# Hymba encoder block: attention and output projection given out in larger groups

## The chip, the cores and the metric

The kernel runs on one core of one Trainium2 chip. The metric is the device time of one execution in microseconds, lower is better; the time before is the median of three runs. The engines are PE (TensorE: matrix products and transposes; its weight loads are shown as PEld), DVE (VectorE), ACT (ScalarE), POOL (GpSimd) and SP (SyncE, which issues most of the DMAs).

## The reference

The reference is one encoder layer over 16 meta tokens and 1024 real tokens of width 1024. Cut to what matters here:

```
u    = rms_norm(h);  proj = u @ w_in            # q, k, v, z of both groups
o_dn = gated delta rule, forward and backward, 4 heads of 128, 16 chunks of 64 and their reversed copy
o_at = softmax(q k^T) v with rope, 8 query heads, 2 key/value heads, head size 64
h    = h + rms_norm(concat(o_dn, o_at) @ w_out) # the output projection
h    = h + rms_norm(square(relu(rms_norm(h) @ w_up)) @ w_down)
```

The output is h without the meta tokens, in float32.

## The kernel before

All values are kept at about float32 accuracy by writing an operand as a high and a low part: a product is then three matmuls (high by high, high by low, low by high). The program is written out in one long order, and each engine runs its own instructions strictly in that order, so the order in which Python emits the work is the schedule.

The order of everything up to the feed-forward part is made by a small planner, `progress` (L1538). Each piece of work is a generator; a `yield` is a place where the planner may go over to another one. The planner keeps a clock `T.t` that counts only matmuls and transposes (the class `Clock`: columns / 2400 us, four times that for float32). After a yield a generator is due again at `T.t` plus the number that it yielded, or plus its entry in `LAT` (L79: chain 2.2, wout 2.4, qk 0.2, pv 0.2, u2 0.22, proj 0.18 us). Of those that are due the first in the list `URGENCY` (L74) is taken: chain0, chain1, wout, wload, then the spawned `post` pieces, then qt, qk, pv, u2, proj, wup. If none is due, the clock jumps to the first that will be.

The generators around the change:

- `chain` (L1065, twice, for the two directions): the recurrence of the delta rule, 8 steps each. A step has five groups of four float32 products of 128x128, each of which waits for what DVE or ACT made of the one before.
- `qk_head` (L1243), driven by `qk_stream` (L1193): the scores of one head of one 128-row tile, S = 128x1024, as two halves of 512 columns, each a product with KH and one with KL. S has `SB` = 2 buffers in PSUM. Then DVE takes the minimum of S (L1254), and the spawned `softmax` (L1259) lets ACT make the exponential (L1262) and the high part in float16 (L1268), POOL and DVE the low part (L1270, L1271), and SP transposes both by DMA into pT (L1274, `PTB` = 3 buffers). No more than `INF` = 6 heads are under way, and a head's scores come at least `TS_` = 2.55 planner us behind the second last one's.
- `pv_head` (L1284), driven by `pv_stream` (L1204) at least `TP_` = 13.8 planner us behind the scores: for each of 8 key tiles three float16 matmuls of 64 or 65 columns into the PSUM tile o, so 24 for a head, with yields behind the third and the sixth key tile (9, 9 and 6 matmuls). Behind every fourth head 12 more for the meta tokens, then DVE divides (L1309, L1310). There are 64 heads in all (8 tiles of 8).
- `proj_stream` (L1387): for each of 8 tiles of 128 rows, `mix` (L1364) transposes the attention's rows (AQ) and the delta rule's (on) on PE, one tile ahead; then two halves of 512 columns with 24 matmuls each by `mm3` (L250), which yields behind every second of its eight triples (6 matmuls). ACT squares the sums (L1406), DVE scales them (L1414), adds x (L1415), and `norm_rows` makes the next layer's rows u. `mix` of a tile waits for the tile's eight attention heads.
- `u2_stream` (L1477) starts when the last attention tile is done. It has 23 pieces of four transposes each (`u_part`, L1430), which turn the rows u and their sums and differences into the operands of the feed-forward products; five of them for each pair of tiles wait for the later tile's projection. Their row loads (L1444) stand in SP's queue.
- `wout_stream` (L1334) loads and splits w_out's first half behind the end of both chains; the projection starts behind it.

Behind the planner comes the feed-forward part, written as a fixed loop, in which PE has matmuls of 512 columns without a break.

Of the kernel before, what the change touches and what calls it, by code (L numbers as in the profile page):

```python
# [81 lines left out]
def body(tc, I, out, dbg=None):  # L82
# [29 lines left out]
    def tmp(dt=F32):  # L112
        return tp.tile([P, LT + 4], dt, name="t4", tag="t4")

    def psr():
        return psa.tile([P, 512], F32, name="a", tag="a")
# [4 lines left out]
    def small(n, name, bufs=4):  # L121
        return sp.tile([P, n], F32, name=name, tag=name, bufs=bufs)

    def junk():
        return sp.tile([P, D], BF16, name="junk", tag="junk", bufs=1)

    def bc(ap, m):
        return ap.unsqueeze(2).broadcast_to([ap.shape[0], ap.shape[1], m])
# [28 lines left out]
    def rsqrt(dst, src, mult, add, n):  # L157
        r = dst.shape[0]
        ms = sp.tile([P, 16], F32, name="ms", tag="ms", bufs=4)
        V.tensor_scalar(ms[:r, :n], src, float(mult), float(add), ALU.mult, ALU.add)  # L160
        G.tensor_tensor(dst, ms[:r, :n], mhalf[:r, :n], ALU.pow)  # L161
# [14 lines left out]
    def mark(name, after=0.0):  # L176

        done[name] = T.t + after
# [71 lines left out]
    def mm3(ps, pairs, every=100):  # L250

        n = len(pairs)
        for i, (ah, al, bh, bl) in enumerate(pairs):
            T.matmul(ps, lhsT=ah, rhs=bh, start=i == 0, stop=False)
            T.matmul(ps, lhsT=ah, rhs=bl, start=False, stop=False)
            T.matmul(ps, lhsT=al, rhs=bh, start=False, stop=i == n - 1)
            if (i + 1) % every == 0 and i + 1 < n:
                yield
# [5 lines left out]
    def norm_rows(dst, X, r, nrow):  # L264
        ss = small(1, "ss")
        A.activation(junk()[:r], X, AF.Square, accum_out=ss[:r])
        rs = small(1, "rs")
        rsqrt(rs[:r], ss[:r], 1.0 / D, EPS, 1)
        V.scalar_tensor_tensor(dst, X, rs[:r, 0:1], nrow[:r], ALU.mult, ALU.mult)  # L269
# [14 lines left out]
    def spawn(name, g):  # L284

        def w():
            yield from g
            live.remove(name)
        live.append(name)
        at = next((i for i, s in enumerate(st) if s[0] in ("gemm", "qt", "qk")), len(st))  # L290
        st.insert(at, [name, w(), LAT[name], 0.0, 0])
# [584 lines left out]
    def need(*names):  # L876
        while not all(n_ in done for n_ in names):
            yield True
        t = max(done[n_] for n_ in names)
        if t > T.t:  # L880
            yield t - T.t
# [322 lines left out]
    def pv_stream():  # L1204
        for n, (t, h) in enumerate(HEADS):
            while len(tq) <= n:
                yield True
            yield until(tq[n] + TP_)
            while h not in boxes[t]:
                yield True  # L1210
            yield from pv_head(h, boxes[t])
            tp_.append(T.t)
# [30 lines left out]
    def qk_head(t, h, qs, sm, mm, box):  # L1243
        kv = h // 4
        ap_, KH, KL = R["at"], R["KH"], R["KL"]
        s = R["ps"].tile([P, L], F32, name="S", tag="S", bufs=SB)
        for half in range(2):
            sl = slice(half * 512, (half + 1) * 512)
            for i, K_ in enumerate((KH, KL)):
                T.matmul(s[:, sl], lhsT=qs[:, h], rhs=K_[:, kv, sl], start=i == 0, stop=i == 1)  # L1250
            if half == 0:
                yield
        mx, nb = small(1, "mx"), small(1, "nb")
        V.tensor_reduce(mx, s, AX.X, ALU.min)  # L1254
        V.tensor_scalar(nb, mx, mm[:, h:h + 1], UP15, ALU.min, ALU.add)  # L1255
        spawn("post", softmax(t, h, s, sm, nb, box))
        yield

    def softmax(t, h, s, sm, nb, box):  # L1259
        yield SM[0]  # L1260
        p32 = tmp()
        A.activation(p32[:, :L], s, AF.Exp, bias=nb, scale=-1.0)  # L1262
        g, j = divmod(h, 4)
        pm = R["PM"][(2 * t + g) % 3]
        A.activation(pm[:, j * NM:(j + 1) * NM], sm[:, h * NM:(h + 1) * NM], AF.Exp, bias=nb, scale=-1.0)
        yield SM[1]
        p16 = R["P16"][(t * NQ + h) % P16N]
        A.copy(p16[:, 0], p32[:, :L])  # L1268
        yield SM[2]
        G.tensor_tensor(p16[:, 1, :LH], p32[:, :LH], p16[:, 0, :LH], ALU.subtract)  # L1270
        V.tensor_tensor(p16[:, 1, LH:], p32[:, LH:L], p16[:, 0, LH:], ALU.subtract)  # L1271
        yield SM[3]
        pT = R["at"].tile([P, 16, P], F16, name="pT", bufs=PTB)
        S.dma_start_transpose(pT, p16.rearrange("p a b -> p (a b)"))  # L1274
        box[h] = pT
        if j == 3:
            ps = psr()[:, :P]
            T.transpose(ps, pm, idf)
            mh, ml = (R["at"].tile([P, P], F16, name=n, bufs=2) for n in ("pmh", "pml"))
            A.copy(mh, ps)  # L1280
            V.tensor_tensor(ml, ps, mh, ALU.subtract)
            box["m", g] = mh, ml

    def pv_head(h, box):  # L1284
        VP, VM = R["VP"], R["VM"]
        t, pT, osb = box["t"], box.pop(h), box["osb"]
        kv, j = divmod(h, 4)
        W = 1 + HD
        if j == 0:
            box["o"] = R["ps"].tile([P, 512], F32, name="o", tag="o", bufs=1)  # L1290
        ob = box["o"][:, :4 * W]

        def term(o, ph, pl, v, first, last):
            T.matmul(o, lhsT=ph, rhs=v[:, :W], start=first, stop=False, skip_group_check=True)
            T.matmul(o[:, 1:], lhsT=ph, rhs=v[:, W:], start=False, stop=False, skip_group_check=True)
            T.matmul(o, lhsT=pl, rhs=v[:, :W], start=False, stop=last, skip_group_check=True)

        for k in range(NT):
            term(ob[:, j * W:(j + 1) * W], pT[:, k], pT[:, 8 + k], VP[:, k, kv], j == 0 and k == 0, False)
            if k in (2, 5):  # L1300
                yield
        if j == 3:
            while ("m", kv) not in box:
                yield True
            mh, ml = box.pop(("m", kv))
            for i in range(4):
                term(ob[:, i * W:(i + 1) * W], mh, ml, VM[:, kv, i], False, i == 3)
            ov, den = ob.rearrange("p (h c) -> p h c", h=4), box["den"][:, h - 3:h + 1]
            V.reciprocal(den, ov[:, :, 0])  # L1309
            V.tensor_tensor(osb[:, h - 3:h + 1], ov[:, :, 1:], bc(den, HD), ALU.mult)  # L1310
        if h == NQ - 1:
            mark(f"att{t}", 2.5)
        yield
# [48 lines left out]
    WORD = (4, 5, 6, 7, 0, 1, 2, 3)  # L1362
# [24 lines left out]
    def proj_stream():  # L1387
        mixes = {}
        yield from need("wout", "att0")
        mixes[0] = mix(0)  # L1390
        yield
        wout, npost = R["wout"], R["npost"]
        for c in range(NT):
            if c + 1 < NT:
                yield from need(f"att{c + 1}")
                mixes[c + 1] = mix(c + 1)
                yield
            mh, ml = mixes.pop(c)
            xr = tmp()
            S.dma_start(xr[:, :D], x[c * P:(c + 1) * P])  # L1400
            s2, pso = small(2, "s1", 2), []
            for n in range(2):
                sl = slice(n * 512, (n + 1) * 512)
                pso.append(psr())
                yield from mm3(pso[n], [(mh[:, k], ml[:, k], wout[k][0][:, sl], wout[k][1][:, sl]) for k in WORD], 2)
                A.activation(junk()[:, sl], pso[n], AF.Square, accum_out=s2[:, n:n + 1])  # L1406
                yield
            rs = small(1, "rs")
            V.tensor_tensor(rs, s2[:, 0:1], s2[:, 1:2], ALU.add)
            rsqrt(rs, rs, 1.0 / D, EPS, 1)  # L1410
            hx = tmp()
            for n in range(2):
                sl = slice(n * 512, (n + 1) * 512)
                V.scalar_tensor_tensor(hx[:, sl], pso[n], rs[:, 0:1], npost[:, sl], ALU.mult, ALU.mult)  # L1414
            V.tensor_tensor(hx[:, :D], hx[:, :D], xr[:, :D], ALU.add)  # L1415
            A.dma_start(hscr[c * P:(c + 1) * P], hx[:, :D])
            if c == 0:
                yield from need("gain")
            norm_rows(xr[:, :D], hx[:, :D], P, R["npre"])
            if c < 6:  # L1420
                A.dma_start(uscr[c * P:(c + 1) * P], xr[:, :D])
            else:
                held[c] = xr
            mark(f"u{c}", 4.0)
            yield
# [406 lines left out]
    for i in range(7):  # L1832
# [17 lines left out]
        for p in range(together):  # L1850
            n = i * NP_ + p
# [39 lines left out]
```

## Time and profile before

| what | value |
|---|---|
| median of 3 runs | 1415.5 us (1413.3 to 1420.03) |
| the profiled execution | 1416.07 us, its span 1414.2 us |
| granted TensorE clock, mean of the span | 0.979 |
| PE busy | 1342.7 us (95%) |
| DVE, ACT, POOL busy | 1029.3 us (73%), 835.5 us (59%), 295.4 us (21%) |

The span is 1.9 us shorter than the execution, which has a start and an end around it. The stages can be told by what PE works on: input projections, convolutions and the inverses of the delta rule up to about 430 us, the chain together with attention up to about 586 us, attention alone while w_out is loaded up to about 616 us, the output projection together with the rest of attention up to about 748 us, the last of the projection to 774 us, a passage to the feed-forward part up to about 806 us, and that part to the end. A matmul's length in the timeline is its time through the array; matmuls overlap, so the time that one costs PE is read from its start to the start of the next.

### The profile page before, as it was taken

The numbers are of one execution on the slowest core, as the hardware profiler recorded it, in microseconds if no ns is written. First come the engines' busy times: TensorE is split into PE (matmuls) and PEld (weight loads), VectorE is DVE, ScalarE is ACT, GpSimd is POOL, SyncE is SP. The second block draws the span as 40 slices with busy tenths as digits, with TensorE's granted clock in tenths as the row PEclk, the third lists the DMA queues.
The fourth block names the chain that finished last, engine by engine and source line by source line (L and its number), as shares of the span: only waits on it lengthen the run. The fifth ranks groups of instructions, "written<-read, shape, count | busy, mean of one in ns | idle before, by whom it ended". The sixth has DMA issues, their size and how long they took to land. (4 is left out here: it accounts for less than half of the span.)

```text
span 1414.2 us, 26476 instructions
## 1 busy us (share of the span) xinstructions
PE 1342.7 (95%) x9627; PEld 1027.1 (73%) x9627; DVE 1029.3 (73%) x1962; ACT 835.5 (59%) x1747; POOL 295.4 (21%) x386
## 2 busy tenths in 40 slices
PE   6999999999998998899998799999999999999996
PEld 6999888777998877677777444444444888888875
DVE  5636779788768979877765987777775588675675
ACT  6556565756546777866644676666665455445552
POOL 1210234343534456533321200000000000000000
PEclk9999999999998999889999799999999999999998
DMA  6312234344379999997994354444443984466341
GB/s 209 87 57 62 83 98 158 112 149 153 121 253 282 245 264 239 221 242 186 224 225 135 102 175 158 153 155 150 158 155 114 331 271 127 142 193 194 98 150 66
DMA packets 273355, 236.86 MB, mean 167 GB/s; under 512 B 147484, under 2 KB 201656, under 8 KB 273224
## 3 DMA queue, kind: packets, MB, share of 16 engines
q1 hardware_dynamic: 270056, 225.73, 55.3%
q10 hardware_dynamic: 3168, 9.44, 1.8%
q8 instruction: 76, 1.25, 0.4%
q14 instruction: 55, 0.45, 0.1%
HBM read 132.27 MB, written 69.28 MB: 143 GB/s over the span
## 5 line engine op out<-in xcount | busy, mean ns | idle before, releaser
L95 PEld LDWEIGHTS <-wh 128*128 128x128 f16 x896 | 88.1, 99 | 102.7 <-issue 1.9
L95 PE MATMUL a<-woah 128*128 128x512 f32 x672 | 158.6, 390 | 1.3 <-DVE woah L1734 1.2
L95 PE MATMUL a<-woal 128*128 128x512 f32 x672 | 157.4, 389 | 0.0
L95 PEld LDWEIGHTS a<-woah 128*128 128x128 f32 x672 | 125.9, 188 | 29.0 <-DVE woah L1734 2.0
L95 PEld LDWEIGHTS a<-woal 128*128 128x128 f32 x672 | 126.1, 188 | 26.2
L95 PE MATMUL a<-uh,wh 128*128 128x344 f32 (+2 forms) x340 | 122.3, 360 | 0.7 <-ACT cw L665 0.5
L1270 POOL TENSOR_TENSOR P<-t,P 128x640 f16<-128x640 f32 x64 | 99.4, 1555 | 106.8 <-ACT P L1268 85.0
L95 PE MATMUL a<-ul,wh 128*128 128x344 f32 (+2 forms) x340 | 118.7, 349 | 0.5 <-DVE ul L262 0.5
L95 PE MATMUL a<-uh,wl 128*128 128x344 f32 (+2 forms) x340 | 118.3, 348 | 0.0
L161 POOL TENSOR_TENSOR rs<-ms,mhalf 128x1 f32<-128x1 f32 (+1 forms) x33 | 19.1, 578 | 424.0 <-DVE rs L1797 304.6
L1254 DVE TENSOR_REDUCE mx<-S 128x1 f32<-128x1024 f32 x64 | 77.9, 1219 | 24.3 <-PE S L95 24.1
L1262 ACT ACTIVATE t<-S,nb 128x1024 f32<-128x1024 f32 x64 | 71.5, 1117 | 40.8 <-DVE nb L1255 29.2
L95 PEld LDWEIGHTS <-pT 128*128 128x128 f16 x1536 | 59.5, 100 | 42.0 <-issue 26.6
L95 PE MATMUL o<-VP,pT 128*128 128x65 f16 (+1 forms) x1536 | 73.6, 198 | 11.3 <-DMA pT<-P 9.8
L95 PEld LDWEIGHTS <-wl 128*128 128x128 f16 x448 | 43.9, 98 | 54.1 <-issue 1.7
L1731 ACT ACTIVATE woah<-fr,isf 128x512 fp32r<-128x512 f32 x54 | 39.2, 725 | 70.3 <-PE a L95 61.0
L1731 ACT ACTIVATE woal<-fr,isf 128x512 fp32r<-128x512 f32 x54 | 39.2, 726 | 68.4 <-PE a L95 66.2
L1268 ACT CAST P<-t 128x1024 f16<-128x1024 f32 x64 | 66.8, 1043 | 4.7 <-DVE t L269 1.8
L1733 DVE SCALAR_TENSOR_TENSOR woah<-fr,isf,woah 128x512 fp32r<-128x512 f32 x54 | 40.5, 751 | 37.2 <-ACT woah L1731 37.1
L95 PE MATMUL S<-KH,qs 128*128 128x512 f32 x128 | 61.0, 476 | 6.5 <-ACT t L1262 6.5
L95 PEld LDWEIGHTS a<-uh,wh 128*128 128x128 f32 x340 | 65.0, 191 | 2.5 <-ACT cw L665 0.7
L95 PEld LDWEIGHTS a<-ul,wh 128*128 128x128 f32 x340 | 65.1, 192 | 2.1 <-DVE ul L262 1.0
(508 smaller groups left out, 3776.8 us busy)
## 6 DMA issues: line engine op xcount, KB each, us to landing
fr<-fscr SPq DMA_DIRECT2D x108, 256.0 KB
fscr<-os SPq DMA_DIRECT2D x64, 256.0 KB
rb<-in_w_down SPq DMA_DIRECT2D x64, 256.0 KB
fscr<-of SPq DMA_DIRECT2D x48, 256.0 KB
wr<-in_w_in SPq DMA_DIRECT2D x44, 256.0 KB
AQ<-in_w_up SPq DMA_DIRECT2D x22, 512.0 KB
raw<-in_w_up SPq DMA_DIRECT2D x10, 512.0 KB
X<-in_x SPq DMA_DIRECT2D x8, 512.0 KB
```

The lines of the kernel that those rows point to most:

```text
L95: nc.tensor.matmul(out, lhsT=lhsT, rhs=rhs, **kw)
L161: G.tensor_tensor(dst, ms[:r, :n], mhalf[:r, :n], ALU.pow)
L1254: V.tensor_reduce(mx, s, AX.X, ALU.min)
L1262: A.activation(p32[:, :L], s, AF.Exp, bias=nb, scale=-1.0)
L1268: A.copy(p16[:, 0], p32[:, :L])
L1270: G.tensor_tensor(p16[:, 1, :LH], p32[:, :LH], p16[:, 0, :LH], ALU.subtract)
L1731: A.activation(ah, fr, AF.Copy, scale=isf[:, p:p + 1])
L1733: V.scalar_tensor_tensor(al, fr, isf[:, p:p + 1], ah.bitcast(F32), ALU.mult, ALU.subtract)
```

## The change

Three lines go or change, all of them places where the planner may go over to other work. The scores of a head lose the yield between their halves, so that their four matmuls of 512 columns come in one go. The values of a head lose the yields behind the third and the sixth key tile, so that their 24 matmuls come in one go. The projection yields behind every fourth triple instead of every second one, so that its matmuls come in twelves. No instruction is added, removed or altered; their order changes, also on the other engines and in the DMA queues, since the planner decides anew at every yield.

```diff
@@ qk_head
             for i, K_ in enumerate((KH, KL)):
                 T.matmul(s[:, sl], lhsT=qs[:, h], rhs=K_[:, kv, sl], start=i == 0, stop=i == 1)
-            if half == 0:
-                yield
         mx, nb = small(1, "mx"), small(1, "nb")
@@ pv_head
         for k in range(NT):
             term(ob[:, j * W:(j + 1) * W], pT[:, k], pT[:, 8 + k], VP[:, k, kv], j == 0 and k == 0, False)
-            if k in (2, 5):
-                yield
         if j == 3:
@@ proj_stream
-                yield from mm3(pso[n], [(mh[:, k], ml[:, k], wout[k][0][:, sl], wout[k][1][:, sl]) for k in WORD], 2)
+                yield from mm3(pso[n], [(mh[:, k], ml[:, k], wout[k][0][:, sl], wout[k][1][:, sl]) for k in WORD], 4)
```

## Rows read from the trace of the kernel before

**Rows 1.** Busy time of each engine by stage; columns as the header says

```profile
core 0: us, PE busy (x) PEld busy (x) DVE busy (x) ACT busy (x) POOL busy (x), PEclk, DMA share, GB/s
436.00:586.00 150.00, 137.85 (x1570) 120.10 (x1569) 131.51 (x287) 111.49 (x239) 82.56 (x61) 0.97 1.08 242
586.00:616.00 30.00, 23.53 (x242) 18.57 (x239) 24.22 (x38) 23.78 (x36) 13.84 (x11) 0.72 1.08 261
616.00:748.00 132.00, 124.20 (x1159) 94.94 (x1155) 88.70 (x163) 75.10 (x130) 42.16 (x34) 1.00 0.90 214
774.00:806.00 32.00, 19.17 (x94) 13.47 (x93) 29.29 (x48) 20.88 (x40) 10.26 (x9) 0.73 0.24 82
```

**Rows 2.** PE's timeline in the projection: start us, us, instruction, count [idle before <-releaser]

```profile
701.99 0.45 PE L95 MATMUL o<-VP,pT 128*128 128x65 f16 x9
702.27 0.48 PE L95 MATMUL a<-woah,mh 128*128 128x512 f32 x1
702.59 0.40 PE L95 MATMUL a<-woal,mh 128*128 128x512 f32 x1
...
703.75 0.36 PE L95 MATMUL o<-VP,pT 128*128 128x65 f16 x6
...
706.17 0.48 PE L95 MATMUL S<-KH,qs 128*128 128x512 f32 x1
706.49 0.40 PE L95 MATMUL S<-KL,qs 128*128 128x512 f32 x1
706.73 0.45 PE L95 MATMUL o<-VP,pT 128*128 128x65 f16 x9
```

**Rows 3.** PE's timeline: first and last of the runs of values' matmuls

```profile
455.52 1.50 PE L95 MATMUL o<-VP,pT 128*128 128x65 f16 x24
...
744.46 0.90 PE L95 MATMUL o<-VP,pT 128*128 128x65 f16 x24
```

**Rows 4.** ACT's group of exponentials, 586 to 616 us: count | busy us, mean ns | idle before

```profile
L1262 ACT ACTIVATE t<-S,nb 128x1024 f32<-128x1024 f32 x8 | 8.9, 1110 | 2.3 <-DVE nb L1255 1.8 <-POOL P L1270 0.5
```

**Rows 5.** ACT's groups of a head, 616 to 748 us

```profile
L1262 ACT ACTIVATE t<-S,nb 128x1024 f32<-128x1024 f32 x22 | 24.6, 1116 | 20.0 <-DVE nb L1255 12.3 <-issue 2.1 <-DVE ml L1378 1.8
L1268 ACT CAST P<-t 128x1024 f16<-128x1024 f32 x23 | 24.0, 1042 | 3.4 <-DVE t L269 1.8 <-DVE ml L1378 1.6
L1265 ACT ACTIVATE PM<-sm__9520,nb 128x16 f32<-128x16 f32 x8 | 2.4, 302 | 0.2 <-DVE nb L1255 0.2
```

**Rows 6.** Waits, 424 to 780 us: total us, times, longest

```profile
PE o L95 <- DMA pT<-P: 9.8, 8, 2.4
...
PE a L99 <- DVE t L1414: 5.1, 5, 1.5
```

**Rows 7.** PE's timeline at two tile boundaries and the projection's end

```profile
731.39 0.66 PE L99 MATMUL a<-c_id,on 128*128 128x128 f32 x4 [0.85 <-DVE t L1414]
...
747.31 0.66 PE L99 MATMUL a<-c_id,on 128*128 128x128 f32 x4 [1.33 <-DVE t L1414]
...
752.54 0.60 PE L99 MATMUL a<-c_id,urow 128*128 128x128 f32 x4
...
773.65 0.40 PE L95 MATMUL a<-wobh,ml 128*128 128x512 f32 x1
773.89 1.47 PE L99 MATMUL a<-c_id,urow 128*128 128x128 f32 x12
781.04 3.65 PE L99 MATMUL a<-c_id,urow 128*128 128x128 f32 x16 [5.68 <-DVE urow L1455]
```

**Rows 8.** DVE's and SP's timelines behind the projection's end

```profile
777.15 1.41 DVE L1414 SCALAR_TENSOR_TENSOR t<-a,rs,npost 128x512 f32<-128x512 f32 x2 [0.18 <-POOL rs L161]
785.09 0.68 DVE L1438 TENSOR_TENSOR t2l<-a,t2h 128x512 f16<-128x512 f32 x1
785.69 0.68 DVE L1438 TENSOR_TENSOR t1l<-a,t1h 128x512 f16<-128x512 f32 x1
763.14 21.89 SPq L1444 DMA_DIRECT2D urow<-uscr  x8
```

## The prediction

> **What bounds the kernel now.** I read the windows by stage first, then PE's timeline, then the waits. The change acts where attention runs, so the reader looks at the stages and not at the shares of the whole span. In [rows 1] the third column is the stretch's length and the next is PE's busy time. With the chain beside attention (436 to 586 us) PE is busy 137.85 of 150 us and DVE 131.51 (88%), two engines close to full. While attention is alone (586 to 616) PE is busy only 23.53 of 30, at a mean granted clock of 0.72. With the projection beside attention (616 to 748) PE is busy 124.20 of 132 and every other engine under 70%: there PE's own work is the bound. In the passage (774 to 806) DVE is busy 29.29 of 32 us and PE only 19.17.
>
> PE's timeline shows what its work costs and that going over between kinds has a price. In [rows 2] the second projection matmul starts at 702.59 and what follows the sixth at 703.75: five steps in 1.16 us, 0.232 us each. The first one behind a run of values starts at 702.27 and the next at 702.59, 0.32 us; the first scores matmul behind such a run also takes 0.32 us (706.17 to 706.49). So a float32 matmul directly behind the short float16 ones costs PE 0.085 us more. The way back is nearly free: nine values' matmuls take 0.28 us (701.99 to 702.27), 0.031 each.
>
> **The first term: fewer goings-over.** I counted the runs of values' matmuls (the stretches of PE's timeline with nothing else between); [rows 3] are the first and the last of 137, and nearly every one has float32 work behind it. By place, 61 end with the chain beside, 9 with attention alone, 67 with the projection. Of the 128 places inside the 64 heads where the planner may go over, it has used most. Without them a head is one run; some heads will follow each other directly. By the heads whose values fall in each stretch I expect about 34 runs beside the chain, 8 alone and 23 beside the projection. That is 27 fewer and 44 fewer. The halves of the scores, now together, also come less often directly behind the chain's short float32 products, which cost the following matmul about the same; I put that at 8 fewer beside the chain. The price is then (27 + 8) x 0.085 = 3.0 us beside the chain and 44 x 0.085 = 3.7 us beside the projection. Beside the chain DVE is nearly as full as PE, so I count half, 1.5 us; beside the projection nine tenths, 3.4 us. Sum -4.9 us. The ends: nothing, if each gain is waited away, and 128 x 0.085 = -10.9 us, if every place paid before and all of it shows.
>
> The Trainium skill ("TensorE: Matmul & The Clock Gate", section "Step-by-step: what each phase is for") says that the next tile's weights load while this tile's matmul runs, since PE pulls the loads ahead. By that alone going over is free and the first term is 0; [rows 2] agree for a long matmul behind a long one and not for the first behind a run of short ones.
>
> **The second term: the order beside the projection.** The projection is last in the list, so it fills what attention leaves. Before, a head's values took three turns, and between two of them the 0.2 us wait let in six projection matmuls or the scores of another head: in [rows 2] the second turn of one head is at 701.99 and that of the next at 706.73, with twelve projection matmuls between. After, values and scores take one turn each, and the projection gets in only when neither is due. The limit is then six heads per loop of 13.8 + 0.65 + 0.85 + 0.4 planner us, plus up to one projection group of 2.56: 15.7 to 18.3, so 2.6 to 3.0 per head. Attention will draw ahead of the projection by some two tiles, and the last tiles are projected alone. PE's sum does not change by this, but its gaps do. At the end of a tile the next `mix` needs a PSUM bank that DVE L1414 must first read; five waits of this kind cost 5.1 us [rows 6], 0.85 and 1.33 of it at the last two [rows 7], with values' matmuls lying beside. Without attention the wait is bare: from the last projection matmul's end (773.65 + 0.40) to the end of DVE's first half at 777.15 + 0.70 [rows 7, 8] are 3.8 us, less some 0.5 for the four transposes that go first: 3.3. Two such waits cost 6.6 - 2.2 = +4.4 us, a third one +1.8 more; the pieces of u2, which stand ahead of the projection in the list and are then under way, fill part of it. I take +2; the ends are 0 and +6.2.
>
> **The third term: the passage.** u2 starts when the last attention tile is done, and only one piece of it fits between two projection groups. Before, 7 of its 23 pieces lay ahead of the projection's end, the first at 752.54, and 16 behind; [rows 7] show the first three of these, twelve transposes at 773.89, and the next four, sixteen transposes at 781.04, which waited 5.68 us for DVE. A piece costs DVE 0.60 us (785.09 to 785.69) [rows 8], in a passage where DVE is full. If attention ends two tiles earlier, u2 starts earlier and about 10 pieces lie ahead: -1.8 us, and the row loads, which hold SP's queue for 21.89 us ahead of the weights' load [rows 8], end sooner. If attention doesn't end earlier, the halved number of turns leaves two more pieces behind, +1.2, or up to +3 with SP's queue. I take -2; the ends are -5 (all of pair and single pieces up to the last but one tile ahead, some eight at 0.6) and +3.
>
> **Costed at nothing.** The chain's products are due first in the list but can't break into a longer turn: 24 values' matmuls last 0.75 us against 0.28, four scores 0.94 against 0.47. That puts the chain later by at most some 0.2 us at each of seven turns in eight steps, 12 us of planner time; attention's heads fill it on PE, so it costs nothing as long as they do. If DVE is too full to let them, up to +9 us (the 12 less the first term's 3). The waits of values for pT, 9.8 us in eight times [rows 6]: pT's three buffers come free sooner, since a head's values no longer lie in three parts, but the heads also follow faster; 0, from -9.8 to the slower case below. SP's queue has the same transposes in the same order of heads. ACT, DVE and POOL do the same work.
>
> **Sum.** -4.9 + 2 - 2 = -4.9 us against the profiled execution, 1416.07, gives 1411.2. That execution is 0.6 us above the median of 1415.5, so the forecast is 1410.6 us. Its own range, with the first two terms half as large or half as large again, is 1406 to 1415.
>
> **Rivals.** *The price of going over comes back as waiting.* For it: DVE at 88% beside the chain, and 13.8 planner us from scores to values, which a faster PE makes shorter in true time. Against it: beside the projection no other engine is near full. It gives 1415.5, within 1413 to 1418. The page's rule above leads to the same time by another way, through a first term of 0.
>
> *Everything pays.* Most of the 128 places (-9), the pT buffers sooner (-3), the passage shorter (-3), the boundaries filled by u2 (0): -15, so 1400.5 us. For it: pT's waits are there to be had, and 5.68 us of waiting in the passage. Against it: the passage hangs on the last tile's own norm, which no order shortens.
>
> *Slower: attention packed too closely.* The place is 616 to 700 us. There a head costs ACT 1.116 + 1.042 + 0.302 = 2.46 us [rows 5], and 22 heads in 132 us leave it idle for long. After, heads come every 2.6 to 3.0 planner us, some 2.9 to 3.3 in true time, and ACT also has the projection's work. From the point where heads in the list come closer than ACT serves them, PE stands at S or pT with ready projection matmuls queued behind, as where attention is alone: 30 - 23.53 = 6.5 us idle for 8 heads [rows 1, 4], 0.81 per head. With the 18 heads whose scores start behind the projection's first group, +14.6 us, and with the first term -4.9: +9.7, so 1425 us. Against it: 0.4 to 0.8 us per head of room.
>
> **Chances.** Forecast 0.41, price waited away 0.20, everything pays 0.21, slower 0.18. About 0.5%, 7 us, is what a measurement of this kernel can tell from no change: under 1408.4 is faster, over 1422.6 slower. Faster has all of "everything pays" and 0.15 of the forecast's lower part, 0.36; slower has 0.16 of its own 0.18; 0.48 is left for no change. The range goes from 1400 to 1422: it leaves out half of each far case.
>
> **What would show it.** The first term: in PE's timeline values in runs of 24 or more, some 65 runs in place of 137, and scores in fours. The second: the last attention tile ends well ahead of 745 us, and projection groups without attention follow, with bare waits for L1414 of about 3 us at their boundaries. The third: more than seven u2 pieces ahead of the projection's end, which comes at about 769 us. The rival of waiting: as few runs, but more PE idle time at pT and S. The prediction is wrong if the projection ends later than at 774 us, or if the passage of 32 us changes by more than 5.

## The result and the profile after

| | us |
|---|---|
| before, median | 1414.74 (1413.3 to 1420.03) |
| after, median | 1432.35 (1429.16 to 1437.32) |
| ratio, 95% interval | 1.0117 [1.0096, 1.0138] |
| profiled execution after | 1432.18, its span 1430.4, granted clock 0.974 |

The median before is that of four runs; 1415.5, from which the forecast was made, is that of the first three. The change makes the kernel some 17 us slower, with an interval wholly above 0.5%; 1410.6 was forecast, and 1400 to 1422 doesn't hold it. The profiled spans differ by 16.2 us. In its line numbers, and in those of the runs without both yields, what stood behind L1252 is 2 lower than before and what stood behind L1301 is 4 lower.

Windows by stage of the kernel after, cut at its own boundaries (columns as in [rows 1]): the chain with attention, attention alone, the projection with attention, the passage.

```profile
436.00:603.00 167.00, 147.11 (x1724) 132.55 (x1723) 150.27 (x306) 126.31 (x256) 90.07 (x67) 0.95 1.06 237
603.00:648.00 45.00, 33.81 (x398) 27.76 (x398) 38.65 (x63) 33.55 (x57) 18.82 (x15) 0.80 1.01 223
648.00:728.00 80.00, 75.40 (x704) 60.44 (x703) 51.44 (x88) 42.36 (x75) 26.16 (x21) 0.99 1.00 224
790.00:818.00 28.00, 13.95 (x77) 9.83 (x78) 23.57 (x43) 19.22 (x37) 9.06 (x8) 0.87 0.29 94
```

Against [rows 1] the first stretch is 17 us longer, and DVE is busy 90% of it (before 88%). Attention ends 17 us earlier (728.4, before 745.7), the projection 15.6 later (789.6, before 774.0). The planner's order says why: 168 of the 256 scores matmuls stand ahead of the chain's end (138), and 191 of the 384 projection matmuls behind the last attention (95). The change has moved 30 scores matmuls, 7.5 heads, from beside the projection to beside the chain.

PE's timeline of the kernel after, in the projection:

```profile
702.42 0.91 PE L95 MATMUL o<-VP,pT 128*128 128x65 f16 x24
703.16 0.48 PE L95 MATMUL a<-wobh,mh 128*128 128x512 f32 x1
703.48 0.39 PE L95 MATMUL a<-wobl,mh 128*128 128x512 f32 x1
703.71 0.39 PE L95 MATMUL a<-wobh,ml 128*128 128x512 f32 x1
```

A head's values are one run, and the first float32 matmul behind them still takes 0.32 us (703.16 to 703.48) as in [rows 2]. The runs fell from 137 to 69.

Waits of PE, 424 to 800 us, kernel after:

```profile
PE o L95 <- DMA pT<-P: 13.7, 7, 3.6
PE a L99 <- DVE t L1410: 5.8, 6, 1.8
PE o L95 <- DVE AQ L1306: 4.0, 3, 1.5
PE a L95 <- DVE den L1305: 2.9, 1, 2.9
```

No one wait grew by much: pT by 3.9 us against [rows 6], the tile boundary (L1410, before L1414) by 0.7, and several new ones of 1 to 3 us on DVE have come. In the chain's stretch alone the waits put down to DVE add up to 12.0 us (430 to 603), against 2.9 before (430 to 583). The longest shows what such a wait looks like. PE's timeline there, kernel after:

```profile
533.83 0.39 PE L95 MATMUL S<-KL,qs 128*128 128x512 f32 x1
537.07 1.44 PE L95 MATMUL a<-idr,t 128*128 128x128 f32 x8 [2.85 <-DVE den L1305]
```

DVE's timeline over the same time:

```profile
533.45 1.21 DVE L1252 TENSOR_REDUCE mx<-S 128x1 f32<-128x1024 f32 x1
534.58 0.54 DVE L1269 TENSOR_TENSOR P<-t,P 128x384 f16<-128x384 f32 x1
535.05 0.20 DVE L1253 TENSOR_SCALAR nb<-mx,mmx 128x1 f32<-128x1 f32 x1
535.17 1.75 DVE L1223 TENSOR_TENSOR t<-AQ,t 128x512 fp32r<-128x512 f32 x1
536.85 0.17 DVE L1305 RECIPROCAL den<-o 128x4 f32<-128x4 f32 x1
```

POOL's, over the same time:

```profile
534.70 1.68 POOL L1268 TENSOR_TENSOR P<-t,P 128x640 f16<-128x640 f32 x1 [1.26 <-ACT P L1266]
536.34 1.72 POOL L1099 TENSOR_TENSOR O<-O,Oprev 128x512 f32<-128x512 f32 x1
```

While PE stands, DVE goes from one instruction to the next without a gap; all of it is attention's work, while the chain's next products (`st` by `QT`, 538.31) stand queued on PE behind the waiting matmul. The longest of DVE's instructions there, L1223, takes 1.75 us, with POOL at work all the while; in the kernel before it took 0.68 us each of its six times between 430 and 620 us (the last section comes back to this).

A tile boundary without attention, PE's timeline of the kernel after:

```profile
744.29 0.66 PE L99 MATMUL a<-c_id,on 128*128 128x128 f32 x4 [1.81 <-DVE t L1410]
745.64 0.58 PE L95 MATMUL a<-woah,mh 128*128 128x512 f32 x1 [0.69 <-DVE t L1410]
746.03 0.63 PE L95 MATMUL a<-woal,mh 128*128 128x512 f32 x1
746.45 0.63 PE L95 MATMUL a<-woah,ml 128*128 128x512 f32 x1
```

The windows ahead of it, behind it and later (columns as in [rows 1], the last but two is the granted clock):

```profile
736.00:744.00 8.00, 6.48 (x35) 5.22 (x33) 1.52 (x4) 2.54 (x7) 0.54 (x1) 1.00 0.49 164
746.00:749.00 3.00, 3.00 (x8) 2.31 (x7) 2.23 (x4) 1.97 (x4) 0.10 (x1) 0.50 0.39 154
750.00:760.00 10.00, 9.68 (x45) 7.53 (x44) 1.93 (x5) 1.83 (x6) 0.10 (x1) 1.00 0.30 107
```

The two waits are 2.5 us, and behind them the granted clock is 0.50, the lower of its two levels (1.2 GHz): matmuls start 0.42 us apart (746.03 to 746.45) in place of 0.23. By 750 it is back. Between the projection's first and last matmul there was no half clock before, and 8.8 us of it after: 3.4 us from 745.9, 3.4 from 762.9, behind a wait of 1.77 us at the next boundary, and the last 2.0 us of a stretch that began at 646.9, ahead of the projection's first matmul.

**The account.** I cut both traces at five events: the chain's last product, the projection's first, attention's last, the projection's last, the first full feed-forward product with t2h. "Idle" is time with no matmul in the array, "half clock" time at the lower level. PE's work is then length less idle less half of the half-clock time; from 430 us to the last event it fell from 312.0 to 307.5 us, -4.5. Idle rose by 15.4, half clock by 3.5 (+1.7), and the feed-forward part behind came out 3.6 longer: +16.2, the difference of the spans. (That part, the same program throughout, took 608.3 to 612.7 us in all profiles here.) The clock accounts for most of the 3.6. The first window is the start of that part in the kernel after, the second in the kernel before:

```profile
818.00:824.00 6.00, 5.18 (x15) 2.16 (x14) 5.60 (x9) 1.31 (x2) 0.01 (x1) 0.50 0.29 85
806.00:812.00 6.00, 5.79 (x29) 2.91 (x29) 6.00 (x11) 2.75 (x5) 0.00 (x0) 1.00 0.34 100
```

In all it is 6.8 us at half clock from 817.5, an estimated 3.4 us.

| lengths, us | chain | attention alone | projection with it | projection alone | passage | idle | half clock |
|---|---|---|---|---|---|---|---|
| before | 153.0 | 40.7 | 122.0 | 28.3 | 31.1 | 39.2 | 47.8 |
| after | 173.1 | 45.2 | 80.1 | 61.1 | 28.1 | 54.6 | 51.3 |
| late chain | 178.8 | 46.0 | 89.6 | 52.0 | 22.1 | 49.3 | 46.1 |
| early chain | 152.3 | 43.2 | 115.7 | 43.5 | 30.3 | 56.4 | 41.0 |
| behind the chain | 152.7 | 41.9 | 90.9 | 69.3 | 22.6 | 47.2 | 38.1 |
| beside the chain | 175.1 | 45.7 | 94.4 | 45.9 | 25.5 | 57.0 | 47.0 |
| behind it, twelves | 152.5 | 42.3 | 112.9 | 43.5 | 30.2 | 50.7 | 44.4 |
| behind it, threes | 149.8 | 41.3 | 92.3 | 84.7 | 20.2 | 56.1 | 47.8 |
| light DVE, before | 154.9 | 44.1 | 122.6 | 28.3 | 30.0 | 43.3 | 51.3 |
| light DVE, beside | 165.2 | 45.6 | 94.1 | 48.6 | 25.5 | 51.7 | 39.7 |
| no twelves | 174.7 | 44.2 | 69.4 | 82.5 | 22.7 | 55.3 | 64.9 |

Each row is one execution (the lower ones are the experiments below). The order up to the chain's end is the same in before and in four of the experiments with all the work (the projection's groups alone, the three runs behind the chain); PE's idle time in that stretch is 12.2, 16.5, 15.2, 15.2 and 12.9 us, so differences of 3 to 4 us in one row mean nothing. Where more heads stand there (after, late, beside, no twelves) it is 19.9, 17.0, 21.0 and 20.6.

### The profile page after: what moved, and what is told of

Same layout as the page of the kernel before. It is cut to its first block, busy times and chain, and to the rows that moved or that the text cites. A ratio compares the mean times of both kernels' runs of the same rounds, so it can differ in the third digit from the quotient of the medians.

```text
span 1430.4 us, 26444 instructions
## 1 busy us (share of the span) xinstructions
PE 1340.7 (94%) x9627; PEld 1034.7 (72%) x9627; DVE 1039.5 (73%) x1962; ACT 835.6 (58%) x1747; POOL 294.3 (21%) x386
## 5 line engine op out<-in xcount | busy, mean ns | idle before, releaser
L1268 POOL TENSOR_TENSOR P<-t,P 128x640 f16<-128x640 f32 x64 | 96.5, 1509 | 110.7 <-ACT P L1266 82.9
L1252 DVE TENSOR_REDUCE mx<-S 128x1 f32<-128x1024 f32 x64 | 77.5, 1214 | 14.4 <-PE S L95 14.4
L95 PEld LDWEIGHTS <-wl 128*128 128x128 f16 x448 | 43.9, 98 | 55.3 <-issue 1.8
L1727 ACT ACTIVATE woah<-fr,isf 128x512 fp32r<-128x512 f32 x54 | 39.2, 725 | 70.3 <-PE a L95 61.0
L1727 ACT ACTIVATE woal<-fr,isf 128x512 fp32r<-128x512 f32 x54 | 39.2, 726 | 68.4 <-PE a L95 66.2
L95 PE MATMUL o<-VP,pT 128*128 128x65 f16 (+1 forms) x1536 | 61.2, 198 | 19.0 <-DMA pT<-P 13.7
L95 PEld LDWEIGHTS <-pT 128*128 128x128 f16 x1536 | 55.3, 100 | 32.3 <-DMA pT<-P 19.0
L95 PEld LDWEIGHTS a<-uh,wl 128*128 128x128 f32 x340 | 64.8, 190 | 1.5
```

The costliest lines, as they stand in the source:

```text
L95: nc.tensor.matmul(out, lhsT=lhsT, rhs=rhs, **kw)
L1727: A.activation(ah, fr, AF.Copy, scale=isf[:, p:p + 1])
```

## Experiments

Times are medians; the ratio is to the kernel before on the same chip (medians 1416.9 to 1418.7), with its 95% interval. It isn't the quotient of the two medians and differs from it by up to 0.2%. The expectations use four letters: A, longer turns push the chain back; B, the large groups themselves make PE stand at pT and o; C, in the first four runs that the projection's twelves leave bare boundaries, later that the projection is left to run alone; D, in A's place from the fifth run on, attention is drawn ahead of the chain to where DVE is full.

**The three parts, each alone.**

```diff
-            if half == 0:        # qk_head
-                yield
```

> Of the change only the scores in one go (four matmuls); values in 9, 9, 6 and the projection in sixes as before. Theory A (longer attention turns push the chain back in the list; the projection starts later, attention runs out earlier, its last tiles run bare): a turn of 0.94 us instead of 0.47 delays the chain about as much as the values do, chain end 588 to 595 us, +4 to +8 us. Theory B (the values' turns pack attention closely, so PE stands at pT and at the single o bank): scores alone change neither, -2 to +2 us. Theory C (the projection's twelves leave bare boundaries and a late u2): 0 to -3 us.

Measured: 1421.8 us, 1.0017 [0.9998, 1.0037]. The ten times fall in two groups (four of 1416.2 to 1416.5, six of 1420.6 to 1425.5), so the size stays unclear. The chain ends at 587.1, just short of A's 588.

```diff
-            if k in (2, 5):      # pv_head
-                yield
```

> Of the change only the values in one go (24 matmuls). Runs of values fall from 137 to about 70. Theory A: chain end 590 to 598 us, +6 to +10 us. Theory B: most of the 17 us is here, +10 to +17 us, with PE idle at pT and AQ/den up by over 8 us. Theory C: -3 to -6 us, since the goings-over are saved and nothing else is lost.

Measured: 1426.06 us, 1.0057 [1.0037, 1.0078]: 9.0 us over the median before, in A's range and below B's. The chain ends at 588.7.

```diff
-  ... for k in WORD], 2)         # proj_stream
+  ... for k in WORD], 4)
```

> Of the change only the projection in twelves. The chain and attention beside it are given out as before: chain end 583 us as before in all theories. Theory C: the end of the projection and the passage lose 8 to 17 us here. Theories A and B: -2 to +4 us, as attention draws somewhat ahead of the projection.

Measured: 1420.05 us, 1.0020 [1.0003, 1.0038]. The values' turn is the largest part. Each of the three costs something or nothing, none gains; their sum, 0.94%, is near the whole 1.17%. C in its first form, a loss of 8 to 17 us by the twelves, falls with the third (+3.0 us); the projection's end and the passage moved by 4.9 and 2.4 us in its trace.

**The chain's place.** First the whole change, with the old yields taken only when a chain is due:

```diff
-            if k in (2, 5):
+            if k in (2, 5) and any(s_[0] in ("chain0", "chain1") and s_[3] <= T.t for s_ in st):
                 yield             # likewise in qk_head
```

> The whole change, but the removed yields of scores and values are kept where a chain's piece is due at that moment (then the planner goes over, else not). Theory A: the chain is as early as before (end within 5 us of 583), the projection starts within 5 us of 624, and the time falls from 1432 to 1408 to 1418 us. Theory B: attention is still packed closely behind the chain and the o bank and pT still stop PE: 1424 to 1432 us. Theory C: 1425 to 1432 us, as the projection is unchanged.

Measured: 1429.52 us, 1.0075 [1.0049, 1.0101], outside A's range and inside B's and C's. But A's condition wasn't met: the chain ends at 593.8, and the order still had 148 scores matmuls ahead of its end, probably since the chain is often not due at the yield but within the turn that follows. The run settles little. Next the whole change with the values held further behind the scores:

```diff
-TS_, TP_, CH_, Q0_ = 2.55, 13.8, 6.0, 6.42
+TS_, TP_, CH_, Q0_ = 2.55, 18.0, 6.0, 6.42
```

> The whole change, and TP_ (planner time from a head's scores to its values) 18 instead of 13.8. The written order then has before's balance with the change's groups: 136 scores matmuls ahead of the chain's end (before 138, after the change 168), 95 projection matmuls behind the last attention tile (before 95, after 191), 79 runs of values (137, 69). Theory D (attention, given out faster, moves ahead of the chain and of the projection in the list; where it moves to, DVE and ACT are full and PE stands, and the tiles it leaves run bare): 1411 to 1420 us, PE idle from 430 us to the feed-forward part back near 39 us. Theory B (the groups themselves: PE can't do other work inside a long turn): 1424 to 1432 us.

Measured: 1436.48 us, 1.0131 [1.0105, 1.0158]. The counts came back to 136 and 95, the time didn't; it is over both ranges, so D missed. My reading is that, with six heads under way at most, the longer way throttles attention: where it is alone it takes 48.9 us (before 40.7), and there are 71.7 us of half clock (47.8). No run tests this reading. Then the reverse, a late chain with nothing of the change:

```diff
-LAT = dict(... chain=2.2, ...)
+LAT = dict(... chain=2.6, ...)
```

> The kernel before with nothing of the change; only the chain's planner latency is 2.6 instead of 2.2, so that the chain is later in the list: 166 scores matmuls ahead of its end (after the change 168), 161 projection matmuls behind the last attention tile (after 191, before 95), 126 runs of values. Theory D: the balance alone costs most of the 17 us, 1425 to 1435 us. Theory B: the groups are those of before, 1413 to 1420 us.

Measured: 1428.97 us, 1.0078 [1.0057, 1.0098], with the old small groups throughout (126 runs of values). D's range holds it: a late chain by itself costs most of what the change does, and B can't be the whole. The whole change with an early chain:

```diff
-LAT = dict(... chain=2.2, ...)
+LAT = dict(... chain=1.8, ...)   # on top of the change
```

> The whole change, and the chain's planner latency 1.8 instead of 2.2: 136 scores matmuls ahead of the chain's end as before the change, but 143 projection matmuls behind the last attention tile (before 95, after 191), 74 runs of values, values still 13.8 behind the scores. Theory D: the part that lies beside the chain comes back, 1416 to 1424 us. Theory B: 1426 to 1433 us. If the distance from scores to values decides (pT not ready), it stays at 1426 to 1433 us too while the run with the larger distance falls.

Measured: 1427.88 us, 1.0069 [1.0047, 1.0092]. The chain's stretch is back at 152.3 us and some of the loss is gone, not all: D's range (1416 to 1424) is missed, and B's holds the time. What is left agrees, interval against interval, with the run behind the chain with twelves, below, whose counts it shares (143 projection matmuls alone); what decides against B is the run behind the chain. And the kernel before with an early chain:

```diff
-LAT = dict(... chain=2.2, ...)
+LAT = dict(... chain=2.0, ...)
```

> The kernel before with nothing of the change, the chain's due time 2.0 in place of 2.2 planner us: the chain stands earlier in the order, 118 scores matmuls ahead of its end (before 138). If the place of the chain has a best point, as theory D in its simple form (the later the worse) does not say, this is the other side of it. D in the simple form: -2 to -5 us, since less attention runs where DVE and ACT are full. D with a best point near before's: 0 to +6 us, since the chain's products then wait at PE for DVE with attention queued behind, and more attention is left for the projection's stage.

Measured: 1422.7 us, 1.0036 [1.0023, 1.0050]: slower too. "The later the worse" is too simple; of the three places tried (2.0, 2.2, 2.6) that of before is the best.

**The change by stage.** With small groups while a chain is in the list, then with small groups only after it:

```diff
-            if k in (2, 5):
+            if k in (2, 5) and any(s_[0] in ("chain0", "chain1") for s_ in st):
                 yield             # likewise in qk_head; the next run has "and not any(...)"
```

> The scores' and values' yields are kept while either chain is under way and left out afterwards; the projection keeps groups of six. The written order is that of before up to the chain's end (138 scores matmuls ahead of it), but 209 projection matmuls stand behind the last attention (before 95). Theory D (attention drawn ahead of the chain costs, through full DVE and ACT beside the chain): this kernel has none of that, and beside the projection PE alone is the bound, so about -3 us of goings-over saved, +3 for bare tile boundaries: 0, within -4 to +5 us. Theory C (the projection left to run alone costs): +6 to +9 us, most of what the values' part alone cost, since here even more of the projection runs alone. Theory B (a head's values in one go make PE stand at pT wherever they run): +6 us, in the stretch from the chain's end on.

> The reverse: the scores' and values' yields are left out only while a chain is under way and kept afterwards; the projection keeps groups of six. The written order has 168 scores matmuls ahead of the chain's end, as the whole change has, and 143 projection matmuls behind the last attention. Theory D: the late chain alone brings most of the loss, +8 to +12 us, with the chain's stage over 165 us long and PE idle there up by 5 us or more. Theory C: +3 to +5 us, as 143 lies half way from 95 to 191. Theory B: half of the loss, +6 us.

Measured: behind the chain 1417.85 us, 0.9998 [0.9986, 1.0010]; beside it 1430.32 us, 1.0087 [1.0069, 1.0105]. This is the plainest pair: the same edit, no effect behind the chain and three quarters of the whole loss beside it. The second is just over D's range (12.9 us over the median before), with a stretch of 175.1 us and 8.8 us more of PE idle in it. With 209 projection matmuls behind the last attention and no loss, C is refuted where the chain is undisturbed, and so is B, which wanted +6 us behind the chain. The first of the two with the projection in twelves as well:

> As the run with groups larger only behind the chain, and the projection in twelves too: 143 projection matmuls behind the last attention and the order of before up to the chain's end. Theory D: -3 to +4 us. Theory C: half of the loss, +6 us, as the twelves make boundaries and the passage worse. If this and the run without the twelves come out below the kernel before, the goings-over saved beside the projection are a gain that the whole change gave away beside the chain.

Measured: 1424.79 us, 1.0045 [1.0027, 1.0062], so the twelves do cost here. The table and the order show where: 28 in place of 56 of u2's transposes stand ahead of the projection's end, and the passage takes 30.2 us, not 22.6. Theory D had expected no loss here; this one isn't D's.

**Why beside the chain.** Windows of the chain's stretch, columns as in [rows 1]. The kernel before:

```profile
430.00:583.00 153.00, 140.85 (x1552) 123.91 (x1551) 130.04 (x286) 112.73 (x236) 81.80 (x60) 0.96 1.08 248
```

The run beside the chain:

```profile
430.00:605.00 175.00, 154.00 (x1765) 138.89 (x1764) 152.64 (x314) 130.16 (x266) 90.75 (x67) 0.95 1.03 239
```

The order of before with less DVE work (the first of the light runs below):

```profile
430.00:585.00 155.00, 142.82 (x1554) 125.94 (x1554) 113.27 (x256) 113.24 (x237) 77.75 (x60) 0.94 1.08 246
```

Beside the chain with less DVE work (the second):

```profile
430.00:595.00 165.00, 148.89 (x1766) 133.16 (x1765) 126.50 (x278) 128.89 (x265) 85.78 (x67) 0.99 1.10 253
```

For the 7.5 heads drawn in, the stretch grew by 22 us. PE was busy 13.2 us more in it, which is its price for them (four scores matmuls at 0.232 and some 27 values' at 0.031 are 1.8 us a head, 13 in all); DVE was busy 22.6 us more, as much as the stretch grew. PE's waits there say the same. The kernel before, its largest on DVE and the one for pT:

```profile
PE a L95 <- DVE rr L1090: 2.0, 1, 2.0
PE o L95 <- DMA pT<-P: 7.0, 6, 2.1
```

Beside the chain, the largest:

```profile
PE S L95 <- ACT t L1262: 4.8, 4, 1.7
PE o L95 <- DMA pT<-P: 3.6, 2, 2.4
PE a L95 <- DVE t L1223: 3.6, 3, 1.7
PE a L95 <- DVE den L1309: 2.9, 1, 2.9
```

All waits put down to DVE are 2.9 us before, 2.6 to 3.2 in three experiments of the same order (the projection's groups alone, behind the chain with sixes and with twelves), 10.2 beside the chain and 12.0 after the whole change. Waits for ACT rose too (1.9 to 7.1 us), and ACT's busy time by 17.4 us, so the light runs take DVE's work away and leave ACT's:

```diff
+        if t * NQ + h < P16N:
             V.tensor_tensor(p16[:, 1, LH:], p32[:, LH:L], p16[:, 0, LH:], ALU.subtract)
```

> The kernel before, but from the fifth head on DVE's part of the low half (L1271, 384 of 1024 columns, 0.82 us a head beside the chain) is left out, so those columns of P's low half keep an old head's values. The written order stays: 138 scores matmuls ahead of the chain's end. It is the base for the next two. DVE as the price beside the chain: about 35 heads there give DVE 29 us back, of which PE, itself 92% busy, can take a few: -4 to -10 us. If DVE is not what holds that stretch: within 2 us of before.

> The same work left out, with the yields left out only while a chain is under way (168 scores matmuls ahead of the chain's end, 143 projection matmuls behind the last attention). To be set against the run above, not against the kernel before. With all of DVE's work this pair of orders differed by 12.4 us. DVE as the price of a head drawn ahead (30 scores matmuls are 7.5 heads; DVE's busy time beside the chain rose by 22.6 us for 22 us of length): with 0.8 us or more of a head's 2.6 to 3 us of DVE gone, the pair differs by +2 to +6 us. The place in the order, pT or ACT as the cause: the pair still differs by +10 to +13 us.

> The same work left out, with the whole change. Against the run of the order before with the same work left out: with DVE as the price +6 to +11 us (what the twelves cost behind the chain stays, about 6, and the rest shrinks); with the place, pT or ACT as the cause +15 to +18 us as with all the work.

Measured, against the kernel before with all its work: order before 1423.13 us, 1.0029 [1.0014, 1.0044]; beside the chain 1422.77 us, 1.0035 [1.0020, 1.0051]; whole change 1426.13 us, 1.0050 [1.0031, 1.0069]. With DVE's full work the first two orders differ by 0.87%, now by 0.06%, where each ratio is uncertain by some 0.15%; the whole change's loss falls from 1.17% to 0.21%.

That is the direction that DVE as the price demands, but all three expectations missed. The light kernel with the order before was to gain 4 to 10 us and lost 4. The pair was to differ by 2 to 6 us and the whole change by 6 to 11; they differ by less than 1 and by 3. Of the 0.81% by which the pair's difference shrank, 0.29% is the order before getting slower. Its chain's stretch is no shorter, and PE's waits for pT are longer (16.9 us from 430 to 629, against 9.8 with all the work from 430 to 624). Why less work makes it slower I can't say; the pair is a comparison within the light kernels.

The lengths of the stretch settle little: it grows by 10 us in the light pair and by 22 with all the work, but the clock differs. The light order before has 17.2 us of half clock in its stretch and the light run beside the chain 3.4 (with all the work 13.6 and 17.1), an estimated 9 of the 12 us between. PE's idle time and waits are plainer. Idle rises from 12.2 to 16.1 us in the light pair and from 12.2 to 21.0 with all the work (12.2 to 16.5 in the runs with the order of before). Waits put down to DVE rise from 1.6 to 2.0 and from 2.9 to 10.2, those for ACT from 2.7 to 5.3 and from 1.9 to 7.1. The place in the order is the same in both pairs. pT comes sooner in the light ones, since the transposes also wait for L1271; but with all the work PE waits for pT less in the late order than in the old one (3.6 us, 7.0 before), so that isn't it. What is left is DVE's time, with a part that may be ACT's. DVE's idle time ahead of the minimum says it in one line each (groups of the chain's stretch; count | busy us, mean ns | idle before). The kernel before:

```profile
L1254 DVE TENSOR_REDUCE mx<-S 128x1 f32<-128x1024 f32 x34 | 41.3, 1217 | 13.3 <-PE S L95 13.2
```

Beside the chain:

```profile
L1254 DVE TENSOR_REDUCE mx<-S 128x1 f32<-128x1024 f32 x42 | 50.8, 1215 | 5.1 <-PE S L95 5.1
```

Beside the chain with less DVE work:

```profile
L1254 DVE TENSOR_REDUCE mx<-S 128x1 f32<-128x1024 f32 x42 | 51.1, 1219 | 19.0 <-PE S L95 18.9
```

Before, DVE still waited 13.2 us for scores; the drawn heads use up that slack, and then PE waits for DVE.

Behind the waits stands the clock. Over all executions its mean is 0.9815 in the kernel before (21 on that chip), 0.9814 behind the chain (12) and 0.9767 beside it (6). Of some 1417 and 1431 us that leaves 26 and 33 us of full clock not granted, so up to about half of the 13 us of loss may be half clock. It is an upper estimate, as some of the half clock falls where PE stands anyway.

**The projection's groups.** Behind the chain as above, with groups of threes:

```diff
-  ... for k in WORD], 2)
+  ... for k in WORD], 1)
```

> All the work; scores' and values' yields left out only behind the chain, and the projection's groups made smaller, threes in place of sixes: 239 projection matmuls behind the last attention, but 80 of u2's transposes ahead of the projection's end (before 28, with sixes 56, with twelves 28). If the groups act through the pieces of u2 that they let in: the passage gets shorter by another 2 to 5 us and the time is -1 to -6 us against before, the first version below it. If they act otherwise (more goings-over, none of them dear between float32 kinds): within 2 us of the run with sixes, which equalled before.

Measured: 1429.79 us, 1.0078 [1.0059, 1.0097], outside both ranges. The passage did get shorter (20.2 us), as expected, but the projection's two stretches take 177.0 us, not 160.2, with 8.8 us more idle and 10 more of half clock. So the pieces of u2 explain the passage and not the time. And the whole change without the twelves:

> Scores and values in one go everywhere, the projection in sixes as before. Its written order has 168 scores matmuls ahead of the chain's end as the whole change has, 245 projection matmuls behind the last attention (191) and 56 of u2's transposes ahead of the projection's end (36). If parts add: the loss beside the chain (+0.87%) plus that behind it (0), so +0.8 to +0.95%, and the twelves then bring the rest of the whole change's +1.17%. If the twelves cost what they did behind the undisturbed chain (+0.47%): +0.7%. If they rather help here, since they hold attention back: above +1.2%.

Measured: 1434.51 us, 1.0120 [1.0101, 1.0138]. PE's waits in its projection:

```profile
PE a L99 <- DVE t L1410: 12.4, 6, 2.5
PE a L99 <- DVE urow L1451: 0.9, 1, 0.9
```

Here attention is furthest ahead (245 projection matmuls alone), the boundaries cost 12.4 us, 6.6 more than after, and the passage 5.4 less. Within the whole change the twelves cost nothing (1.0117 with them). None of the three outcomes expected fits: beside the chain 0.87 and behind it nothing don't add up to 1.20.

No version tried is faster than before; the change behind the chain alone equals it.

## Why the prediction was wrong

**The failing step is "Costed at nothing".** It said that the chain comes later by at most 12 planner us, that attention's heads fill this on PE, and that it costs nothing as long as they do; only if DVE is too full, up to +9. The heads did fill PE, and that was the cost. The chain's end moved 20.1 us (583.0 to 603.1). The run beside the chain alone measured this step at +12.9 us. The warning was at hand in [rows 1]: DVE had 18.5 of the 150 us left beside the chain, and the 7.5 heads brought it 22.6 us; beside the projection, where they came from, it was PE's time that they cost. In numbers of the run beside the chain: 22.1 us longer there, 5.0 where attention is alone (partly the spread of executions), 15.6 shorter from the projection's start on, +11.5. I had named the mechanism and its condition, used it to halve the first term, and then put nothing for it into the sum.

**Term 1, fewer goings-over (-4.9).** Right in the count, 69 runs of values where about 65 were expected, and in the price of one: the first float32 matmul behind a run still takes 0.32 us, the next 0.23. PE's work fell by 4.5 us, close to the forecast, but that doesn't show the size. The same sum gives 308.5 us for the projection's groups alone, which leave the values' yields in, and 316.2 for the late chain with its 126 runs, against 312.0 before; some 4 us come and go with the order. The Trainium skill ("TensorE: Matmul & The Clock Gate", section "Step-by-step: what each phase is for") says that the next tile's weights load while this tile's matmul runs. By that alone the term would be 0; the 0.32 us in both traces speak against it for this one step. Whatever was saved, the idle time ate it.

**Term 2, the order beside the projection (+2, at most +6.2).** Right in direction, too small. Attention ends two tiles of the projection earlier, as said (191 of its 384 matmuls stand behind it, before 95). The waits at the boundaries, which the term counted, rose by only 0.7 us, with pieces of u2 lying among them; no run shows whether these are the reason. But idle time from the projection's start to its end rose by 3.6 us in all, and the half clock behind two of the boundaries, which I had not counted, brings 6.8 / 2 = 3.4. Some +7 in all. In the run behind the chain the projection takes 9.9 us longer than before and the passage 8.5 less.

**Term 3, the passage (-2).** It measured -3.0 (31.1 to 28.1), with 9 pieces of u2 ahead of the projection's end (7 before, about 10 expected).

**The rivals.** The slower one came nearest in time (1425) and had the wrong place: it looked for PE standing at S or pT, with ACT as the limit, beside the projection from 616 to 700 us. Where attention and the projection run together, PE's idle time hardly changed (4.4 us before in 122.0, 4.6 after in 80.1), with no wait for ACT after and 0.7 us at pT. Between 616 and 700 us it did rise, from 5.3 to 9.4 us, but attention alone, which before ended at 623.7, now reaches to 648.3. The condition given in the first rival, DVE at 88% beside the chain, was the true one, but there it could only eat a gain, not turn it. Of the checks named, the end of the projection behind 774 us said that the forecast was wrong (789.6); the passage changed by 3 us, not by more than 5.

**What stays open.** About 0.3% of the whole change is left once the part beside the chain is taken off (1.17 less 0.87, with both intervals some 0.3 uncertain). The run behind the chain with twelves, 0.45%, would fill it: the two add up to 1.32%, within the interval of the whole. But without the twelves the parts don't add up, and boundaries, half clock and passage trade against each other (the twelves cost 0.47% behind an undisturbed chain, 0.20% alone, and nothing within the change). I found no rule for it. Open too are how the price beside the chain divides between DVE and ACT, and why the light kernel is slower in the order of before.

## What to carry to other kernels

When an edit moves work from one stage to another, price it in each stage by the engine that is full there, not by the engine whose instructions were edited. A stage at 88% of DVE has room for a few heads only, and the same head can cost 3.0 us of DVE there and 1.8 us of PE elsewhere. In a schedule made by a list and due times, count in the new order what stands ahead of each stage's end before summing what the edit saves.

## What was not expected of the hardware

DVE's instructions get longer where the stretch is crowded: the low half L1271 took 782 ns on average in the chain's stretch before and 920 in the run beside the chain, the difference of Q (L1223) 682 ns (430 to 620 us) and 1343; this adds to the price of a head (22.6 / 7.5 = 3.0 us of DVE). No run tried the cause, but the traces point to POOL. From 430 to 605 us of the kernel before, 11 of 39 L1271 had less than 0.1 us of POOL's work beside them and took 546 ns (at most 551); the other 28 took 917 on average. Beside the chain 16 without POOL took 544 and 24 with it 1170. None of the six L1223 before had POOL beside it (675 to 693 ns); in the kernel after, the four long ones (1330 to 1754 ns) had POOL at work for 783 to 1792 ns, the two short ones (676 and 684) for 284 and 563. So being beside POOL doesn't always cost, but no long one is without it. Leaving out L1271 also takes these meetings away: in the light run beside the chain L1223 took 681 to 870 ns. And a wait of 2.5 us at a tile boundary was followed by 3.4 us at a granted clock of 0.50, so the boundary cost more than the wait that the profile shows.
